# An mLSTM and HGRN2 decoder layer in one kernel: the mLSTM's fourfold key rows go through DRAM

## The chip, the cores and the metric

The kernel runs on one core of a Trainium2 chip. The metric is device time in microseconds (us), the median of several executions. Before the change it was 2313.5 us (three runs, 2311.78 to 2313.61).

## The reference

One inference step of one decoder layer, for a prompt of 256 new tokens and for 8 sequences of 8 new tokens each (the samples), 320 tokens in all, in float32. Two token mixers run on the same input: an mLSTM with 4 heads (keys of 256, values of 512) and an HGRN2 with 8 heads. Cut to the mLSTM:

```python
def step(carry, xs):
    C, n, m = carry
    ...
    s = jnp.einsum('bhtk,bhsk->bhts', qc, kc) * d
    num = jnp.einsum('bhts,bhsv->bhtv', s, vc) + w_inter[..., None] * jnp.einsum('bhtk,bhkv->bhtv', qc, C)
    den = jnp.sum(s, axis=-1) + w_inter * jnp.einsum('bhtk,bhk->bht', qc, n)
    h = num / jnp.maximum(jnp.abs(den), jnp.exp(-m_t))[..., None]
    ...
    C_new = decay[..., None, None] * C + jnp.einsum('bhs,bhsk,bhsv->bhkv', w_end, kc, vc)
    n_new = decay[..., None] * n + jnp.einsum('bhs,bhsk->bhk', w_end, kc)
    return (C_new, n_new, m_new), h
```

A large input projection stands before the mixers; branch projections, sigmoid gates, an output projection, LayerNorm, a feed-forward net (relu squared, 2048 to 8192 and back) and a second LayerNorm stand behind them. For the change only `C_new` of the samples matters: for each of 8 sequences and each head the sum over its 8 tokens of (weighted key) x (value), a 256x512 matrix.

## The kernel before

**Main stream.** All large products are written as 304 weight tiles of 128 output channels and 2048 input channels (`TILES`), each in two halves ("units", 128x1024 floats). float32 is got from float32r matmuls: a unit is loaded by DMA into `wr` (3 buffers, queue SP), ACT copies it to `wh` (the high part) and DVE subtracts to get `wl` (the low part, L478). Three matmuls (hi x hi, hi x lo, lo x hi) for each 128x128 block make 48 main matmuls a tile, 14592 in all, nearly all from L335 (`mm`). The activations stay in SBUF (`xh`, `xl`).

**Side work.** Everything else is written as Python generators (chains) that yield one instruction at a time with an estimated cost: ("pe", cost, fn), ("dve", ...), ("act", ...), ("sp", ...). A planner (`Sched`) runs while the program is built. It keeps an estimated clock for each engine; after every third main matmul `pump` lets the chains emit what would be ready by that clock. A PE instruction of a chain is emitted only when its inputs are estimated to be ready 450 ns before (`PE_LAT`). Chains wait on events (`Ev`, a planned time) and take buffers from pools (`acq`, `rel`). On the chip every engine, and every DMA queue, then runs its instructions in the order in which they were emitted, and waits on semaphores wherever the data are not there yet. So the plan sets the order; if the chip is later than the plan, an engine stands. All loads and stores but a few are issued by SP through one line (L338): weights (`wr<-wt`), the samples' states in and out (`C`, `Cs`), spills.

**The mLSTM heads.** The tiles of a head come as four value tiles, two key tiles, two query tiles and two gate tiles. They take the first 345 us or so for the four heads. For each head:

- `m_V` transposes the value tiles to token rows (L927). The samples' 64 token rows are split into a high part and a low part (`vs`). Then `copies_to` writes each of them into a DRAM tile `vsDm` twice, at row offset r of each sequence's 32 rows (four DMAs, one for each r), and `copies_from` reads the whole back as `vst`: "fourfold rows", 32 rows for each sequence. The planner books 5.0 us for the writes to land and 6.0 us for the read.
- `m_KW` multiplies the key tiles with the weights W (L979, L981) into `kw`, two tiles of 320 tokens, transposes the prompt's 256 tokens (four transposes, L986) and splits them into `khl` (ACT, then DVE at L991), which `m_CP` writes to DRAM (`kD`, beside `vD` for the values) for the end of the program. Then it sums the samples' keys (L1000 to L1002) and makes the keys' fourfold rows without DRAM: for each of the two key tiles `stack` (ACT and DVE, L950) writes the 64 sample tokens four times beside each other (high, low, high, low) into `st` (128x256), and two transposes (L1012) put them into a PSUM bank, 4 transposes a head. One ACT instruction (128x512) evicts the bank to `kst`, and the event KS is set.
- `m_sample` and `m_update` wait for KS and for `vst`, and make the state sums: `m_sums`, small matmuls (32 rows, 32x512) of `kst` with `vst`, whose 32 rows carry high x high, low x high, high x low and low x low. DVE adds them to the decayed state (L1238), and SP stores it.

`m_KW` of a head waits for KS of the head before; a buffer of `qk` becomes free at S, KS and QW.

Of the kernel before, what the change touches and what calls it, by code (L numbers as in the profile page):

```python
# [8 lines left out]
F32 = mybir.dt.float32  # L9
F32R = mybir.dt.float32r  # L10
# [3 lines left out]
ALU = mybir.AluOpType  # L14
# [8 lines left out]
MH, DK, DV = 4, 256, 512  # L23
# [207 lines left out]
def wait(*evs):  # L231
    return ("wait", evs)


def acq(pool, n=1):
    return ("acq", pool, n)


def rel(pool, item):
    return ("rel", pool, item)  # L240


def post(ev):
    return ("set", ev)


def act(n, psum=False, ptr=0):
    return ((61 if psum else 112) + n) / 1.2 + 93 * ptr


def dve(n, psum=False, mode=1, ptr=0):
    return ((62 if psum else 66) + n / mode) / 0.96 + 55 * ptr
# [10 lines left out]
PE_T = 112.0  # L263
# [28 lines left out]
class Program:  # L292
# [48 lines left out]
    def carve(self):  # L341
        class Part:
            def __init__(self, ap, lo=0):
                self.ap, self.o, self.end = ap, lo, ap.shape[1]

            def __call__(self, n, parts=128):
                self.o += n
                assert self.o <= self.end, (self.o, self.end)
                return self.ap[:parts, self.o - n:self.o]

            def three(self, a, b):
                return self(a * b).rearrange("p (a b) -> p a b", a=a)

        self.Part = Part
        A, B, C, R = Part(self.f1), Part(self.f2), Part(self.f3), Part(self.ra[:, 0:6400])

        self.hs = Pool([A(2048) for _ in range(3)])

        self.qk = Pool([A.three(4, 320) for _ in range(2)])
        self.vr = Pool([A.three(4, 320)])  # L360
        self.kw = Pool([B.three(2, 320)])
        self.bc = Pool([B(712) for _ in range(2)])
        self.eb0 = B(512)
        self.eb = Pool([self.eb0])
        self.stg = Pool([B(256) for _ in range(2)])
        self.qn0 = B(256)
        self.qn = Pool([self.qn0])
        X = Part(self.rx)
        self.cb = Pool([C(512) for _ in range(6)] + [X(512) for _ in range(8)])
        self.hb0 = C.three(3, 512)  # L370
        self.hb = Pool([self.hb0])
        self.qz0 = C(512)
        self.qz = Pool([self.qz0])
        self.tst = Pool([B(320) for _ in range(2)])
        self.tst2 = B(320)
        self.shl = Pool([(R(384), R(384), R(256))])
        self.vhl = Pool([R(2048).rearrange("p (x s v) -> p x s v", x=2, s=2)])
        self.vs = Pool([R(512)])
        self.khl = Pool([R(1024).rearrange("p (x s k) -> p x s k", x=2, s=2)])
        self.kst = Pool([R.three(2, 256)])  # L380
        self.vst = Pool([R.three(2, 512)])

        A, B, R = Part(self.f1, 6144), Part(self.f2), Part(self.rh)
        self.sb = Pool([A.three(4, 256) for _ in range(2)])
        self.at = Pool([A(512) for _ in range(2)])
        self.yb0 = A(1024)
        self.yb = Pool([self.yb0])
        self.it2 = [B.three(3, 256) for _ in range(2)]
        self.it = Pool(self.it2)
        self.hstg0 = [B(128) for _ in range(2)]  # L390
        self.hstg = Pool(self.hstg0)
        self.on0 = B.three(3, 256)
        self.on = Pool([self.on0])
        self.ho = Pool([B(320) for _ in range(2)])
        R2 = Part(self.ra, 5120)
        self.hkst = Pool([R2.three(2, 128)])
        self.phl = Pool([(R2(512), R2(512))])
        self.hvst = Pool([R.three(2, 256)])
        self.late = [B(320) for _ in range(4)]
        self.ats0 = B(128)  # L400
        self.ats = Pool([self.ats0])
        self.sg = Pool([Part(self.f2, 4960)(320), self.tst2])
        B = Part(self.f2, 4304)
        self.sr = Pool([B(320) for _ in range(2)])
        B = Part(self.f2, 3840)
        self.xr = Pool([B(320) for _ in range(4)])
        B = Part(self.f2)
        self.lnb = [B(320) for _ in range(7)]
        self.tmp = Pool([B(320) for _ in range(3)])
# [404 lines left out]
    def m_start(self, h):  # L814
        m = self.mh[h]
        self.qk.free.sort(key=lambda x: x[0])
        m["qk"] = self.qk.free.pop(0)[1]
        for n in ("q", "k"):
            m[n] = [Ev(), Ev()]
        m["v"] = [Ev() for _ in range(4)]  # L820
        for n in ("E", "S", "Vt", "Vs", "KW", "KH", "KS", "N", "CP", "QW", "bc_", "vst", "S0", "C", "ld"):
            m[n] = Ev()
        s = self.s
        s.spawn(self.m_E(h), 2)
        s.spawn(self.m_S(h), 2)
        s.spawn(self.m_KW(h), 3)
        s.spawn(self.m_V(h), 2)
        s.spawn(self.m_num(h), 2)
        s.spawn(self.m_CP(h), 4)
        m["parts"], m["inter"] = ([Ev() for _ in range(2 * NB)] for _ in range(2))  # L830
        m["cbs"] = []
        s.spawn(self.m_sample(h), 3)
        s.spawn(self.m_states(h), 3)
        for name, evs, pool in (("qk", ("S", "KS", "QW"), self.qk), ("eb", ("N", "S0"), self.eb), ("shl", ("N", "S0"), self.shl),
                                ("vhl", ("N", "CP"), self.vhl), ("vs", ("S0", "vst"), self.vs), ("kst_", ("QW", "KS"), self.kst), ("vst_", ("QW", "vst"), self.vst)):
            s.spawn(self.m_done(h, name, evs, pool), 3)

# [99 lines left out]
        m["vst_"] = vst  # L937
        yield from self.copies_from(self.vsDm[h], vst, m["vst"])

    def stack(self, st, src, his):  # L940

        v = self.nc.vector
        w = st.rearrange("p (b r t) -> p b r t", r=4, t=8)
        x = src.rearrange("p (b t) -> p b t", t=8).unsqueeze(2).to_broadcast([128, 8, 2, 8])
        step = his[1] - his[0]
        los = [r for r in range(4) if r not in his]
        pick = lambda rs: w[:, :, rs[0]:rs[0] + 2 * step - (step - 1):step, :]
        hi, lo = pick(his), pick(los)
        yield ("act", act(128), lambda: self.A(hi.bitcast(F32R), x))
        yield ("dve", dve(128), lambda: v.tensor_tensor(lo.bitcast(F32R), x, hi, ALU.subtract))  # L950

    def copies(self, hi, lo, to, his, st, ev):

# [15 lines left out]
    def m_KW(self, h):  # L969
        nc, v, m = self.nc, self.nc.vector, self.mh[h]  # L970
        if h:
            yield wait(self.mh[h - 1]["KS"])
        yield wait(*m["k"], self.rows_ev, m["bc_"])
        qk = m["qk"]
        W = m["bc"][:, 320:640]
        kw = yield acq(self.kw)
        for c in range(2):
            k = qk[:, 2 + c, :]
            yield ("dve", dve(256), lambda: v.tensor_tensor_reduce(  # L979
                kw[:, c, 0:256], k[:, 0:256], W[:, 0:256], 1.0, 0.0, ALU.mult, ALU.add, self.np_o[:, 2 * h + c:2 * h + c + 1]))  # L980
            yield ("dve", dve(64), lambda: v.tensor_tensor(kw[:, c, 256:320], k[:, 256:320], W[:, 256:320], ALU.mult))  # L981
        khl = yield acq(self.khl)
        b = yield acq(self.sbank)
        for i in range(2):
            for c in range(2):
                yield ("pe", PE_T, lambda: nc.tensor.transpose(b[:, 256 * i + 128 * c:256 * i + 128 * c + 128], kw[:, c, 128 * i:128 * i + 128], self.ident))  # L986
        m["khl"] = khl
        kh, kl = khl[:, 0], khl[:, 1]
        bv = b.rearrange("p (a k) -> p a k", a=2)
# [5 lines left out]
        n0, ns = self.n0[:, h], self.ns_o[:, h]  # L995
        sm = yield acq(self.sm)
        tm = sm[:, 0:16].rearrange("p (c b) -> p c b", c=2)
        kv = kw[:, :, 256:320].rearrange("p c (b t) -> p c b t", t=8)
        dc = m["bc"][:, 704:712]
        yield ("dve", dve(128), lambda: v.tensor_reduce(tm, kv, AX.X, ALU.add))  # L1000
        yield ("dve", 90, lambda: v.tensor_tensor(ns, n0, dc.unsqueeze(1).to_broadcast([128, 2, 8]), ALU.mult))
        yield ("dve", 90, lambda: v.tensor_tensor(ns, ns, tm, ALU.add))  # L1002
        yield rel(self.sm, sm)
        kst = yield acq(self.kst)
        m["kst_"] = kst
        b = yield acq(self.sbank)
        bv = b.rearrange("p (g k) -> p g k", g=2)
        for c in range(2):
            st = yield acq(self.stg)
            yield from self.stack(st, kw[:, c, 256:320], (0, 2))  # L1010
            for g in range(2):
                yield ("pe", PE_T, lambda: nc.tensor.transpose(bv[:, g, 128 * c:128 * c + 128], st[:, 128 * g:128 * g + 128], self.ident))  # L1012
            yield rel(self.stg, st)
        yield rel(self.kw, kw)
        yield ("act", act(512, True), lambda: self.A(kst, bv))
        yield rel(self.sbank, b)
        yield post(m["KS"])

    def ln_post(self, h, i, src, den, hb, parts, psum):

# [898 lines left out]
    def run(self, pool):  # L1919
# [10 lines left out]
        self.kD = [self.dr.tile([128, 2, 2, 256], F32, name=f"kD{j}") for j in range(MH)]  # L1930
        rows = lambda name, n, k: [self.dr.tile([32 * NB, k], F32, name=f"{name}{j}") for j in range(n)]
        self.ksD, self.vsD = rows("ksD", HH, HK), rows("vsD", HH, HV)
        self.vsDm = rows("vsDm", MH, DV)
        self.vD = [self.dr.tile([128, 2, 2, 512], F32, name=f"vD{j}") for j in range(MH)]
        self.ln = [dict(c=Ev(), x=Ev(), end=Ev(), pre=Ev(), m=Ev(), fin=Ev(), s=[Ev() for _ in range(KT)]) for _ in range(2)]
        self.xq, self.xq_ev = [None] * KT, [Ev() for _ in range(KT)]
# [83 lines left out]
```

## Time and profile before

| what | value |
|---|---|
| median of 3 runs | 2313.5 us |
| time of the profiled execution | 2313.08 us |
| its span, first to last instruction | 2311.3 us |
| mean granted clock of TensorE | 0.999 |
| DMA, mean rate over the span | 188 GB/s |
| L1012, transposes of the stacked keys | 16, 272 ns median, 75.2 to 331.9 us |
| L986, transposes of the prompt's keys | 16, 271 ns median, 64.0 to 317.9 us |
| DVE waiting for ACT's copies of weights (wl <- wh) | 443.0 us in 391 waits |
| SP waiting for L478 (weight buffers) | 817.8 us in 285 waits |

The page of a profile gives the busy time of each engine (PE is TensorE, PEld its weight loads, DVE VectorE, ACT ScalarE, POOL GpSimd), the chain of work that ended last, followed back from the last instruction, and the costliest groups of instructions by line of the kernel. Idle time of an engine that is off that chain costs nothing. A group's line has the operation, what it writes and reads (out<-in), the shape, how many there were, busy time and mean duration, and after the second bar the idle time ahead of it and what ended it. The views that answer a question add: waits (who waited for whom, how long in all, how often, the longest), stretches of time with each engine's busy time, instructions of one line or tile, and the timeline.

### The profile page before, as it was taken

The page shows a single profiled execution, that of the slowest core. Times are in us where ns is not written, and L with a number is a line of the kernel's source. Part 1 is how long each engine was busy: PE and PEld are TensorE (multiplying, and loading weights), DVE is VectorE, ACT ScalarE, POOL GpSimd, SP SyncE. Part 2 cuts the span into 40 slices and gives each one's busy share as a digit, 9 for nine tenths or more (in the row PEclk, how much of TensorE's full clock was granted, in tenths as well). Part 3 has the DMA queues.
Part 4 walks back from the last instruction along what each step waited for, and adds up shares of the span by engine and source line. Part 5 has one row for each costly group of instructions (what it writes and reads, how often), then busy time and mean ns, then how long its engine had stood idle before and what let it go on. Part 6 is the DMA issues. An engine that isn't in the chain of part 4 may idle for free.

```text
span 2311.3 us, 38984 instructions
## 1 busy us (share of the span) xinstructions
PE 2301.8 (100%) x15704; PEld 2259.0 (98%) x15704; DVE 1387.9 (60%) x2418; ACT 1040.0 (45%) x1649; POOL 12.2 (1%) x44
## 2 busy tenths in 40 slices
PE   9999999999999999999999999999999999999998
PEld 8999999999999999999999999999999999999998
DVE  6566567677777776555555767544554455445555
ACT  5444445454555555444433446533442344234434
POOL 0000000000000000000000000000000000000000
PEclk9999999999999999999999999999999999999999
DMA  6888686665666554555555644444444444444465
GB/s 214 286 303 267 232 302 219 201 216 194 197 201 226 190 193 166 180 172 173 174 170 183 217 158 146 148 153 146 147 153 148 148 151 149 147 149 151 146 228 182
DMA packets 155357, 434.96 MB, mean 188 GB/s; under 512 B 17436, under 2 KB 47268, under 8 KB 154152
## 3 DMA queue, kind: packets, MB, share of 16 engines
q1 hardware_dynamic: 154024, 426.18, 55.0%
q0 software_dynamic: 1152, 6.29, 0.8%
q8 instruction: 123, 2.02, 0.4%
q14 instruction: 58, 0.48, 0.1%
HBM read 376.25 MB, written 56.15 MB: 187 GB/s over the span
## 4 chain that ended last, share of the span: by engine, by line
PE 95%; DMA 2%; ACT 1%; DVE 1%; SPq 0%; issue 0%; ACTq 0%
PE bank L335 94%; DMA wr<-wt 2%; ACT f3m L329 0%; DMA Cs<-f 0%; DVE wl L478 0%; ACT wh L329 0%; PE bank L1602 0%; SPq L338 0%; DVE bb L478 0%; PE bank L1174 0%; ACT bb L329 0%; PE bank L927 0%; DMA f<-C 0%; PE bank L1438 0%; ACT oC L329 0%
## 5 line engine op out<-in xcount | busy, mean ns | idle before, releaser
L478 DVE TENSOR_TENSOR wl<-wr,wh 128x1024 fp32r<-128x1024 f32 x423 | 518.4, 1226 | 444.0 <-ACT wh L329 443.0
L335 PE MATMUL bank<-xh,wh 128*128 128x320 f32 (+1 forms) x2408 | 782.2, 325 | 0.4 <-ACT wh L329 0.4
L335 PE MATMUL bank<-xh,wl 128*128 128x320 f32 (+1 forms) x2408 | 746.1, 310 | 0.5 <-DVE wl L677 0.4
L335 PE MATMUL bank<-xl,wh 128*128 128x320 f32 (+1 forms) x2408 | 743.9, 309 | 0.0
L329 ACT ACTIVATE wh<-wr 128x1024 fp32r<-128x1024 f32 (+1 forms) x428 | 450.9, 1053 | 460.3 <-PE bank L335 432.4
L335 PEld LDWEIGHTS bank<-xh,wh 128*128 128x128 f32 x2408 | 453.8, 188 | 9.0 <-issue 3.4
L335 PEld LDWEIGHTS bank<-xl,wh 128*128 128x128 f32 x2408 | 454.3, 189 | 3.5
L335 PEld LDWEIGHTS bank<-xh,wl 128*128 128x128 f32 x2408 | 453.5, 188 | 1.0 <-DVE wl L677 1.0
L478 DVE TENSOR_TENSOR bb<-wr,bb 128x1024 fp32r<-128x1024 f32 x179 | 219.4, 1226 | 231.7 <-ACT bb L329 231.5
L335 PE MATMUL bank<-xh,bb 128*128 128x322 f32 x1280 | 287.2, 311 | 0.0
L335 PE MATMUL bank<-ra,bb 128*128 128x320 f32 x1264 | 283.6, 309 | 0.0
L329 ACT ACTIVATE bb<-wr 128x1024 fp32r<-128x1024 f32 x179 | 188.8, 1055 | 202.4 <-PE bank L335 191.6
L335 PE MATMUL bank<-rxb,bb 128*128 128x320 f32 x1112 | 255.0, 309 | 0.0
L335 PE MATMUL bank<-ra,wh 128*128 128x320 f32 x892 | 250.0, 309 | 0.0
L335 PEld LDWEIGHTS bank<-xh,bb 128*128 128x128 f32 x1280 | 215.9, 188 | 0.0
L335 PEld LDWEIGHTS bank<-ra,bb 128*128 128x128 f32 x1264 | 210.6, 188 | 0.2
L335 PE MATMUL bank<-xl,bb 128*128 128x322 f32 x640 | 198.7, 310 | 0.0
L335 PEld LDWEIGHTS bank<-rxb,bb 128*128 128x128 f32 x1112 | 188.4, 188 | 0.2
L335 PE MATMUL bank<-rxb,wh 128*128 128x320 f32 x596 | 184.3, 309 | 0.0
L335 PE MATMUL bank<-rxb,wl 128*128 128x320 f32 x596 | 183.9, 309 | 0.0
L329 ACT ACTIVATE f<-f,misc 128x320 f32<-128x320 f32 x210 | 118.0, 562 | 140.4 <-DVE f L1869 128.8
L335 PEld LDWEIGHTS bank<-ra,wh 128*128 128x128 f32 x892 | 161.5, 188 | 1.1 <-DVE ra L1632 0.9
(273 smaller groups left out, 2229.2 us busy)
## 6 DMA issues: line engine op xcount, KB each, us to landing
wr<-wt SPq DMA_DIRECT2D x602, 512.0 KB
rx<-C SPq DMA_DIRECT2D x36, 256.0 KB
Cs<-rx SPq DMA_DIRECT2D x36, 256.0 KB
f<-C SPq DMA_DIRECT2D x28, 256.0 KB
Cs<-f SPq DMA_DIRECT2D x28, 256.0 KB
vD<-ra SPq DMA_DIRECT2D x4, 1024.0 KB
f<-S SPq DMA_DIRECT2D x8, 512.0 KB
f3h<-S SPq DMA_DIRECT2D x8, 512.0 KB
```

The costliest lines, as they stand in the source:

```text
L329: return self.nc.scalar.activation(out, in_, func, **kw)
L335: self.nc.tensor.matmul(*a, **kw)
L478: self.V().tensor_tensor(lo, raw, hi.bitcast(F32), ALU.subtract)
```

## The change

The keys' fourfold rows are made as the values' are. `kw` becomes one tile of 640 columns: prompt tokens of key tile 0, the 64 sample tokens of tile 0, the 64 of tile 1, prompt tokens of tile 1. So the sample tokens of both key tiles are 128 adjacent columns, and one transpose turns them all. It is emitted ahead of the prompt's four. Two ACT copies and two DVE subtractions (each 64 rows of 128) put high and low parts into a new tile `ks` (in a part of `ra` that was not used), a new chain `m_KS` writes them with four DMAs to a DRAM tile `ksDm` and reads `kst` back. `stack`, its buffers `stg`, four transposes and an ACT eviction a head are gone. `m_KW` ends with a new event KW, for which the next head and the `qk` buffer wait in place of KS. Buffers in `f2` lie at other offsets.

```diff
-        self.kw = Pool([B.three(2, 320)])
+        self.kw = Pool([B(640)])
...
-        self.stg = Pool([B(256) for _ in range(2)])
...
+        self.ks = Pool([self.ra[:, 6400:6656]])
...
-    def stack(self, st, src, his):
...
-        yield ("act", act(128), lambda: self.A(hi.bitcast(F32R), x))
-        yield ("dve", dve(128), lambda: v.tensor_tensor(lo.bitcast(F32R), x, hi, ALU.subtract))
+    def pairs(self, src, b, to, n):
+        nc, v = self.nc, self.nc.vector
+        for p in range(n):
+            yield ("pe", PE_T, lambda: nc.tensor.transpose(b[:, 128 * p:128 * p + 128], src[:, 640 * p + 256:640 * p + 384], self.ident))
+        w = to.rearrange("q (p e k) -> q p e k", e=2, k=128)
+        up, dn = slice(0, 64), slice(64, 128)
+        for e, (h, l) in enumerate(((up, dn), (dn, up))):
+            x, hi, lo = b[h, 0:128 * n].rearrange("q (p k) -> q p k", k=128), w[h, :, e, :], w[l, :, e, :]
+            yield ("act", act(128 * n, True), lambda: self.A(hi, x))
+            yield ("dve", dve(128 * n, True), lambda: v.tensor_tensor(lo, x, hi.bitcast(F32), ALU.subtract))
...
     def m_KW(self, h):
         nc, v, m = self.nc, self.nc.vector, self.mh[h]
         if h:
-            yield wait(self.mh[h - 1]["KS"])
+            yield wait(self.mh[h - 1]["KW"])
...
+        ks = yield acq(self.ks)
+        b = yield acq(self.sbank)
+        yield from self.pairs(kw, b, ks, 1)
+        yield rel(self.sbank, b)
+        t = self.s.t["dve"]
+        self.s.spawn(self.m_KS(h, ks), 3, t)
         khl = yield acq(self.khl)
         b = yield acq(self.sbank)
...
-        kst = yield acq(self.kst)
-        m["kst_"] = kst
-        b = yield acq(self.sbank)
-        bv = b.rearrange("p (g k) -> p g k", g=2)
-        for c in range(2):
-            st = yield acq(self.stg)
-            yield from self.stack(st, kw[:, c, 256:320], (0, 2))
-            for g in range(2):
-                yield ("pe", PE_T, lambda: nc.tensor.transpose(bv[:, g, 128 * c:128 * c + 128], st[:, 128 * g:128 * g + 128], self.ident))
-            yield rel(self.stg, st)
-        yield rel(self.kw, kw)
-        yield ("act", act(512, True), lambda: self.A(kst, bv))
-        yield rel(self.sbank, b)
-        yield post(m["KS"])
+        yield rel(self.kw, kw)
+        yield post(m["KW"])
+
+    def m_KS(self, h, ks):
+        m = self.mh[h]
+        yield from self.copies_to(ks[64:128], ks[0:64], self.ksDm[h], (0, 2))
+        yield rel(self.ks, ks)
+        kst = yield acq(self.kst)
+        m["kst_"] = kst
+        yield from self.copies_from(self.ksDm[h], kst, m["KS"])
```

## The prediction

> **What bounds the kernel now.** I read the head of the page first: who is busy, and who is on the chain that ended last.
>
> ```profile
> span 2311.3 us, 38984 instructions
> PE 2301.8 (100%) x15704; PEld 2259.0 (98%) x15704; DVE 1387.9 (60%) x2418; ACT 1040.0 (45%) x1649; POOL 12.2 (1%) x44
> ...
> PE 95%; DMA 2%; ACT 1%; DVE 1%; SPq 0%; issue 0%; ACTq 0%
> ```
>
> TensorE is busy for all but 9.5 us of the span, most of that at the two ends. So time falls only if TensorE gets less to do, and rises only if it has to stand. Next, the waits of PE alone: after the first 26 us the longest is this one.
>
> ```profile
> PE bank L1012 <- DVE f L950: 0.4, 1, 0.4
> ```
>
> It belongs to the code that the change removes. Third, the groups by line, and the chain of waits between 324 and 333 us, for what a transpose really costs.
>
> ```profile
> L1012 PE MATMUL bank<-cst,f 128*128 128x128 f32 x16 | 4.4, 275 | 0.4 <-DVE f L950 0.4
> ```
>
> ```profile
> 327.11 0.11 PE bank L1012
> ...
> 330.40 0.11 PE bank L1174
> 330.51 0.11 PE bank L1012
> ```
>
> A transpose lasts 275 ns by itself, but transposes and matmuls overlap, and the chain charges each with 0.11 us. The timeline of PE shows the same:
>
> ```profile
> 326.65 0.31 PE L335 MATMUL bank<-xl,wh 128*128 128x320 f32 x1
> 326.80 0.31 PE L335 MATMUL bank<-xh,wl 128*128 128x320 f32 x1
> 326.94 0.27 PE L1012 MATMUL bank<-cst,f 128*128 128x128 f32 x1
> 326.97 0.39 PE L335 MATMUL bank<-xh,wh 128*128 128x320 f32 x1
> 327.20 0.31 PE L335 MATMUL bank<-xl,wh 128*128 128x320 f32 x1
> ```
>
> Two main matmuls without anything between them start 0.15 us apart (326.65, 326.80). From 326.80 to 327.20 there are two such steps and one transpose: 0.40 - 0.30 = 0.10 us. I take 0.11.
>
> Fourth, the four stretches in which the mLSTM heads make their keys, for the DMA engines that the change loads, and the DMAs of the value rows, which already go the way that the key rows are to go.
>
> ```profile
> core 0: us, PE busy (x) PEld busy (x) DVE busy (x) ACT busy (x) POOL busy (x), PEclk, DMA share, GB/s
> 58.00:85.00 27.00, 27.00 (x191) 24.95 (x191) 16.11 (x36) 12.18 (x20) 0.00 (x0) 1.00 0.98 363
> 142.00:168.00 26.00, 26.00 (x188) 23.91 (x186) 13.81 (x29) 13.10 (x24) 0.00 (x0) 1.00 0.89 324
> 230.00:256.00 26.00, 26.00 (x187) 23.83 (x186) 13.84 (x29) 12.69 (x24) 0.00 (x0) 1.00 0.76 254
> 312.00:345.00 33.00, 32.63 (x231) 29.84 (x229) 19.72 (x38) 15.26 (x28) 0.00 (x0) 1.00 0.90 319
> ```
>
> ```profile
> L338 SPq DMA_DIRECT2D vsDm<-ra x16: 575/586/1476, 59.6 to 322.8; - x16
> L338 SPq DMA_DIRECT2D ra<-vsDm x4: 371/709/1066, 71.1 to 328.7; - x4
> ```
>
> ```profile
> SPq L338 <- DMA vsDm<-ra: 4.8, 4, 3.9
> ```
>
> PE is full in all four (but for 0.4 us in the last), and the DMA engines nearly so in the first (0.98). The last fence: SP, the queue that issues every weight load, stood 4.8 us in four waits until value rows had landed in DRAM, once for 3.9 us.
>
> **The change part by part.** *Transposes.* Each head loses four at L1012 and gains one: 4 x 3 = 12 fewer, 12 x 0.11 = 1.3 us off TensorE. It is always full, so all of it lies on the path. Bounds: nearest rows of transposes that stand alone between main matmuls run from 0.11 to 0.20 us each, so 1.3 to 2.4. I take 1.3, since the chain charges that in three rows of three.
>
> The Trainium skill (TensorE: Matmul & The Clock Gate, Part 4: PE-mode transpose) gives about 275 ns for a 128x128 transpose inside a kernel. The group's mean here is just 275, but that is how long one lasts. Priced by it, the 12 would bring an estimated 3.3 us; the chain's 0.11 says they don't.
>
> *The stall.* The 0.4 us wait at 325.89 goes with L950: that DVE instruction stood behind a weight split (wl, 324.41 to 325.63) which a late weight load had delayed. In its place the single transpose waits for L981, an instruction after which L986 already transposes today at 314.8 without standing. I take -0.4; from 0 if a neighbour inherits it.
>
> *ACT and DVE.* Out per head: two ACT copies of 128x128 (0.30 us each), one ACT eviction of 128x512 (0.60), two DVE subtractions (0.29). In: two ACT copies and two subtractions of 64x128 from PSUM, 0.27 and 0.29 by the rows of L1491's kind. ACT saves 0.66 us a head, DVE nothing. Both are idle nearly half the time, so 0. The four copies now stand ahead of the prompt's transposes (L986), which move back by some 2 us; behind them are the DMAs to kD and vD, read only at the end of the program. 0. The next head's key work waits for KW, earlier than KS: heads lie over 80 us apart, 0.
>
> *DMAs.* Per head four writes of 64 KB and one read of 256 KB, 0.5 MB. At the 363 GB/s of the first stretch that is 1.4 us of all engines; in the other stretches there is room. They take SP 4 x 0.58 + 0.4 = 2.7 us. Behind them wait weight loads and state loads. What covers them: by the timeline, each weight half is split (end of wl) at least 4.0 us before its first matmul; in the four stretches 4.1 to 9.2. So 2.7 us are hidden, and even 2.7 + 1.4 very nearly. Were the cover gone, they would cost at most 4.1 - 4.0 in the worst place: 0 to 0.1 a head. I take 0.
>
> *The new wait.* The first of the small sums of a head (m_sums, 32x512 matmuls) needs kst, now from DRAM. Time for it, from the head's first key transpose to its first sums: 19.2, 22.5, 22.7 and 23.2 us (63.9 to 83.1, 144.3 to 166.9, 232.7 to 255.4, 314.9 to 338.1). What it needs, by the value rows: some 2.5 for the four copies (1.1 busy and the queueing behind a 1.23 us split), 3.0 to 6.9 from first to last write issue, 4.8 to 7.0 from there to the read, 0.4, and the planner's 6.0 + 0.6 until PE may use it: 17.3 to 23.4, some 20 likely. So in head 0 the key rows are about last, in the others there are some 3 us to spare. That the planner puts sums later costs nothing, as PE gets main matmuls instead. It costs only where the real read is later than planned, for then PE stands, and all main matmuls with it. Bounds: 0, and for a landing of 7.64 us (the longest in the chain here, "DMA Cs<-f" from 310.64) 7.64 - 6.6 = 1.0 a head, 4.2 in all. I take 0, since the value rows' reads (used 4.7 to 12 us after issue) made PE stand nowhere.
>
> Sum: -1.3 - 0.4 = -1.7 us against the profiled execution, whose own time is 2313.08 (span 2311.3 and 1.8 around it): 2311.4. The median of the runs, 2313.5, lies 0.4 above that execution, so 2311.8 is forecast: 0.07% less. No change that is measurable, as I count under 0.2% (4.6 us) as none: it is about what a measurement of this kernel can tell from no change.
>
> **The rivals.** *The gain is taken back.* One or two heads stand for kst by about 1 to 2 us, above all head 0, where the DMA engines are full and spare time is least; the net is -0.7 to +2.5: 2312.8 to 2316. For it: 0.98 share and 17.3 to 23.4 against 19.2. Against: the value rows in the same stretch.
>
> *The key rows come late, slower.* The place is SP's read of ksDm, which waits in the queue until four writes have landed. The planner books 5.0 us. Head 2's value rows took 3.9 more. A read that starts 3.9 us late makes PE stand 3.9 us at the first sums, once the spare time there is used up. Two such heads cost 7.8 - 1.7 = +6.1: 2319.6; all four 15.6 - 1.7 = +13.9: 2327. It decides from 3.2 us of late landing per head in two heads (4.6 + 1.7 = 6.3 us in all). For it: key and value writes now queue together in full DMA stretches, and SP's two waits add up ahead of weight loads with 4.1 us of cover. Against: three of the four waits of today were together 0.9 us, and heads 1 to 3 have some 3 us to spare.
>
> The Trainium skill (DMA: Bandwidth & Descriptors, Anatomy of one DMA) speaks for this rival: completion "can cause a surprisingly long delay especially when the write target is HBM"; its constant is some 2 us. The trace has 4.8 to 7.0 us from last write to read, part of which is the planner's. By that constant alone no head would be late, and 2311.8 would stand.
>
> *More than the count says.* Twice the stall and transposes at 0.2 give 2.4 + 0.8 = 3.2 us, still within 0.2%. Faster by 4.6 us has no place in the trace; what remains is a new order of work that happens to suit.
>
> **How the numbers follow.** Forecast 2311.8: 0.55. Taken back: 0.22. Late key rows: 0.18. More than the count, past 0.2%: 0.05. So faster 0.05, same 0.55 + 0.22 = 0.77, slower 0.18. Range: below, 2.4 + 0.4 off the profiled time gives 2310.3 and I let it reach 2309.8; above, up to the two-headed case, 2319. What is left out is the 0.05 below and about half of the late case.
>
> **What would show it.** Right: one key-row transpose a head in place of four, PE's idle time after 26 us near zero, no row "PE bank <- DMA ra<-ksDm". Taken back: that row with 1 to 2 us at the first sums of head 0 (about 83 us). Late: that row with 3 us or more, and SP waiting for "DMA ksDm<-ra" over 3 us a time. I am wrong if the clock row moves from 1.00, if main matmuls wait for wl, or if the new order of work leaves PE standing far behind the mLSTM heads, which no row here lets me see.

## The result and the profile after

The changed kernel is slower: 2318.85 us, the median of 17 runs (2315.43 to 2323.56), against 2312.58 us for the kernel before in 17 runs beside it (2311.33 to 2313.91). The ratio is 1.0027 with a 95% interval of 1.002 to 1.0033: 4.6 to 7.6 us. Its spread is also three times that of before, 8.1 us against 2.6.

The head of the page after:

```profile
span 2318.0 us, 38988 instructions
PE 2303.0 (99%) x15692; PEld 2260.4 (98%) x15692; DVE 1388.2 (60%) x2418; ACT 1038.3 (45%) x1645; POOL 12.2 (1%) x44
...
PE 97%; DMA 1%; ACT 1%; DVE 0%; issue 0%; SPq 0%; ACTq 0%; DVEq 0%
```

PE has the 12 instructions fewer that the change promised (15704 to 15692), and yet 1.2 us more busy time, and the span is 6.7 us longer. The busy time that is not work but a slower clock is explained below; the rest is standing. The waits of PE (who waited for whom: us in all, times, the longest):

```profile
PE bank L335 <- DMA ra<-ksDm: 3.7, 1, 3.7
PE bank L335 <- ACT wh L329: 2.0, 1, 2.0
PE bank L335 <- DVE f L1733: 1.2, 1, 1.2
```

The first row is new: once, the small sums of a head waited 3.7 us for the key rows from DRAM. The second is at 10 us, the start of the program (0.4 before); it is 1.8 in an experiment below that is not slower, so it belongs to the execution and not to the change. The third is the sum for LayerNorm at 1300 us (L1727 before, 0.3 there). The wait for L950 is gone. The one transpose a head has the length that was expected; instructions of its line:

```profile
L947 PE MATMUL bank<-cst,f x4: 270/272/329, 65.3 to 323.9; 128*128 128x128 f32 x4
```

Where the 3.7 us lie, and what follows them, shows in the timeline of PE in head 1:

```profile
169.14 1.46 PE L335 MATMUL bank<-rx,f 128*32 128x512 f32 x10
174.28 0.80 PE L335 MATMUL bank<-ra 32*128 32x512 f32 x4 [3.69 <-DMA ra<-ksDm]
175.01 0.64 PE L335 MATMUL bank<-xh,wh 128*128 128x320 f32 x1
175.45 0.47 PE L335 MATMUL bank<-xl,wh 128*128 128x320 f32 x1
175.72 0.47 PE L335 MATMUL bank<-xh,wl 128*128 128x320 f32 x1
```

Behind the wait the same main matmuls last 0.47 us where they lasted 0.31, and start 0.27 us apart where they started 0.15 apart. The stretches around it say why (PEclk is the granted clock):

```profile
165.00:170.00 5.00, 5.00 (x41) 3.90 (x40) 3.75 (x7) 3.90 (x9) 0.00 (x0) 1.00 1.03 356
170.00:175.00 5.00, 1.31 (x12) 0.29 (x4) 0.00 (x0) 0.00 (x0) 0.00 (x0) 0.84 1.01 407
175.00:180.00 5.00, 5.00 (x23) 4.86 (x20) 3.29 (x4) 1.06 (x1) 0.00 (x0) 0.50 0.46 169
180.00:185.00 5.00, 5.00 (x35) 4.57 (x34) 3.00 (x5) 3.23 (x6) 0.00 (x0) 0.97 0.82 279
```

Still during the wait TensorE's granted clock falls to a half; by the trace's clock record it stays there from 173.4 to 180.3 us, 6.8 us. Six of them fall on work, which costs some 3.0 us. So the wait costs twice: 3.7 + 3.0 = 6.7 us. The Trainium skill (TensorE: Matmul & The Clock Gate, Why this matters for your kernels) warns of just this: no gaps over some 3 us between matmuls. The trace agrees at 3.69 us; the limit itself is tried below.

The chain of waits names what led up to it (start, us, what), and SP's timeline the order of the DMAs:

```profile
160.77 4.71 DMA ksDm<-ra
...
165.86 8.38 DMA ra<-ksDm
```

```profile
163.24 0.42 SPq L338 DMA_DIRECT2D wr<-wt  x1
163.77 0.40 SPq L338 DMA_DIRECT2D kD<-ra  x1
164.22 0.52 SPq L338 DMA_DIRECT2D vD<-ra  x1
165.86 0.37 SPq L338 DMA_DIRECT2D ra<-ksDm  x1
```

The last key write took 4.7 us to land, within the 5.0 booked. The read took 8.38 us from issue to landing, where the planner books 6.0 and PE's 0.6 on top. Right ahead of it SP had issued kD and vD, 1.5 MB, which at the 400 GB/s of this stretch are 3.8 us of all DMA engines.

The slow landing alone would not have made PE stand. In the same planned piece of PE's work (`m_sample`, booked as `PE_C`, 2.0 us) other products stand ahead of the sums; in the trace they take from 168.67 to 170.60. So the plan left the read at least 0.62 for its issue, 6.0, 0.6 and 1.9, some 9.1 us, between its issue and the sums. PE was there 4.74 us after the issue (170.60 less 165.86). By these bookings SP issued the read at least 4.4 us late against PE, and it is both together that make 3.7: 4.4 + 8.4 - 9.1. With a landing of 5.0 the same sum leaves 0.3. Where SP lost its time is not settled: between 138 and 170 us it stood 6.0 us for stores of states to land (`Cs<-rx`; 2.5 in the kernel before), but 6.6 in experiment 8, where PE does not stand.

Laying the n-th main matmul of one trace beside the n-th of the other gives the balance: the changed kernel is 1.0 us behind at 34 us (the start), 0.9 at 155, 6.2 at 676, 5.7 at 1290 and 6.5 at 1308 us. Head 1's wait and the clock make up the step in the middle (+6.7, less some 1.4 saved on transposes and the old stall), and 0.8 is lost at LayerNorm (0.2 in the second profile, experiment 11).

### The profile page after: what moved, and what is told of

Read it like the earlier page. It is cut to its first block, busy times and chain, and to the rows that moved or that the text cites. A ratio compares the mean times of both kernels' runs of the same rounds, so it can differ in the third digit from the quotient of the medians.

```text
span 2318.0 us, 38988 instructions
## 1 busy us (share of the span) xinstructions
PE 2303.0 (99%) x15692; PEld 2260.4 (98%) x15692; DVE 1388.2 (60%) x2418; ACT 1038.3 (45%) x1645; POOL 12.2 (1%) x44
## 4 chain that ended last, share of the span: by engine, by line
PE 97%; DMA 1%; ACT 1%; DVE 0%; issue 0%; SPq 0%; ACTq 0%; DVEq 0%
PE bank L335 96%; DMA wr<-wt 0%; ACT f3m L329 0%; DMA ra<-ksDm 0%; PE bank L1608 0%; PE bank L927 0%; PE bank L1180 0%; DMA ksDm<-ra 0%; PE bank L1444 0%; ACT oC L329 0%; SPq L338 0%; DVE bb L478 0%; ACT wh L329 0%; PE bank L996 0%; PE bank L1557 0%
```

## The experiments

The theory: the key rows' read lands later than it is booked, PE stands in the order of the plan, and the clock falls. The rivals: the added DMA traffic costs time by itself; or the new order of work does.

**1. The booking alone.** One number of the planner:

```diff
-        yield from self.copies_from(self.ksDm[h], kst, m["KS"])
+        yield from self.copies_from(self.ksDm[h], kst, m["KS"], 11000.0)
```

(`copies_from` books that in place of 6000.)

> The changed kernel, with one number of the planner different: it books 11 us instead of 6 for the read of the key rows. Theory (PE stands in head 1 because the read lands 8.4 us after its issue where 6.0 are booked, and TensorE's clock then falls to a half for 6.8 us): no wait of PE for ksDm, granted clock 1.00 throughout, and about 2311 to 2312.5 us, 0 to 2 below the kernel before. Rival (the added DMA traffic or the new order costs time whatever PE waits for): still some 4 us or more above the kernel before.

Measured: 2314.21 us against 2313.23 for the kernel before (ratio 1.0002, interval 0.9993 to 1.0011). No wait for ksDm is left, and the clock stays at 1.00. The loss is gone, within that interval, with no DMA and no instruction taken away: what cost time was the wait, with the clock's fall behind it. The median lies 1.7 us above the upper end of what I expected, so the gain isn't there either.

**2. kD and vD behind the read.**

```diff
-        yield wait(m["KH"], m["Vt"])
+        yield wait(m["KH"], m["Vt"], m["KS"], m["vst"])
```

> The changed kernel, with the writes of kD and vD (1.5 MB a head) planned after the fourfold rows have come back. Theory (in head 1 the read stands behind these 1.5 MB on the DMA engines, 3.8 us at the 400 GB/s moved there): the read lands within the 6 us booked, PE does not wait for ksDm, 2311 to 2312.5 us. Rival (the read is late because of the weight and state loads around it, or because SP issues it late): PE still waits 2 us or more for ksDm in some head, and the time stays at 2315 or more.

Measured: 2312.45 us (ratio 1.0, interval 0.9991 to 1.0009). No wait for ksDm in the profile, at the old booking of 6 us. Two of 11 runs were at 2317, though. A read that is late now and then would explain them, but no trace of such a run was kept; experiment 3, whose sums need no key rows from DRAM, has one at 2317.75 too, and the kernel before reaches 2315.9 in the runs beside it. Its waits of PE begin with

```profile
PE bank L335 <- DVE f L1733: 1.0, 1, 1.0
```

which is the LayerNorm sum again, taken up in experiment 8.

**3. The traffic alone.** In the kernel before, a chain beside `m_KW` writes 64 rows of `khl` four times and reads 256 KB back into a tile that nothing uses:

```diff
+    def m_X(self, h):
+        x = self.mh[h]["khl"][:, 0, 0, :]
+        yield from self.copies_to(x[64:128], x[0:64], self.ksDm[h], (0, 2))
+        yield from self.copies_from(self.ksDm[h], self.spare, Ev())
...
+        self.s.spawn(self.m_X(h), 3, self.s.t["dve"])
```

> The kernel before, its key rows still made by four transposes a head, with DMAs of the changed kernel's shapes added (four writes of 64 rows of 1 KB to DRAM, one read of 256 KB back into a tile that nothing reads). Theory (the traffic itself is covered; only the wait costs): 2312.5 to 2314, within 1 us of the kernel before, no new wait of PE over 0.5 us. Rival (traffic in full DMA stretches delays weights and states): 4 us or more slower, with PE or the weight splits waiting for loads.

Measured: 2312.66 us (ratio 0.9999, interval 0.999 to 1.0008). SP even waited 15.8 us for these writes to land (us in all, times, the longest), and no wait of PE names a load:

```profile
SPq L338 <- DMA ksDm<-ra: 15.8, 5, 5.9
```

The first rival falls: the 0.5 MB a head and SP's 2.7 us are covered, as the prediction had it.

**4. The price of a transpose.** In the kernel before, each transpose of L1012 is issued four times (`for _ in range(4)`).

> The kernel before, each of its 16 transposes of stacked keys issued four times in place of once: 48 more transposes, nothing else. Theory (a transpose takes 0.11 us of the stream on PE): 5.3 us slower, 2317.9. Rival (it takes the 0.27 us that it lasts): 13 us slower, 2325.6.

Measured: 2318.27 us, 5.04 above the kernel before (ratio 1.0023, interval 1.0014 to 1.0032). That is 0.105 us for each of the 48 (0.07 to 0.15 by the interval), not 0.27. By this, 12 fewer are worth 1.3 us.

**5. A booking in between.** As 1, with 8000.0.

> The changed kernel with 8 us booked for the read of the key rows, between the 6 of the change and the 11 of e1_book11. Theory (PE stands for what the read takes beyond the booking, and the clock falls only after a long stand): a wait of PE for ksDm of 1 to 2.5 us in head 1 or none, granted clock 1.00 throughout, and 0 to 2 us over e1_book11. Rival (any stand costs a fixed price, or the wait does not follow the booking): a wait of 3.5 us or more, the clock at a half for some 6 us, 2317 or more.

Measured: 2314.87 us (ratio 1.001, interval 1.0 to 1.0019), with seven runs from 2314.3 to 2315.3 and three from 2318.8 to 2319.2. The profile is of one of the three, and shows two waits, 0.53 us in head 1 and one in head 3:

```profile
348.37 0.80 PE L335 MATMUL bank<-ra 32*128 32x512 f32 x4 [3.08 <-DMA ra<-ksDm]
```

With it the clock went to a half from 348.1 for 6.8 us. I had expected no wait over 2.5 us and no fall of the clock, and missed: in head 3, where the read stood behind kD and vD as well, it took 9.0 us from issue to the sums. The two groups of runs, 4 us apart, fit a wait that comes in some executions; only the one profile shows it.

**6. Standing on purpose.** In the kernel before, in the feed-forward part: a matmul, n fills by GpSimd, a matmul that needs them, for n from 1 to 12.

```diff
+            self.mm(b[:, 0:1], x[:, 0:128], one, start=True, stop=True)
+            for _ in range(n + 1):
+                pool.memset(x[:, 0:640], 1.0)
+            self.mm(b[:, 1:2], x[:, 0:128], one, start=True, stop=True)
```

(The code counts its n from 0.)

> The kernel before, with twelve stands of TensorE made on purpose in the feed-forward part, where weights lie ready 20 us ahead: a small matmul, then n fills of a tile by GpSimd (128x640, some 0.6 us each), then a small matmul that needs them, with n from 1 to 12, some 56 us apart. Theory (TensorE's clock falls to a half only after a stand of between 0.5 us, which the kernel before has without a fall, and 3.7 us, and stays low for some 6 us once it works again): short stands show a clock of 1.00 and cost their own length, long ones a stretch at 0.5 and some 3 us more. Rival (the halved clock of the changed kernel had another cause): clock 1.00 throughout and about 55 us longer, the sum of the stands.

Measured: 2396.19 us, 82.8 above the kernel before, where PE stood for 55.2 us in all. The timeline for n of 1, 2, 3, 5 and 12 (PE's idle time in brackets):

```profile
1513.77 0.38 PE L335 MATMUL bank<-misc,f 128*128 128x1 f32 x2 [0.80 <-POOL f L613]
...
1572.20 0.38 PE L335 MATMUL bank<-misc,f 128*128 128x1 f32 x2 [1.50 <-POOL f L613]
...
1633.11 0.38 PE L335 MATMUL bank<-misc,f 128*128 128x1 f32 x2 [2.19 <-POOL f L613]
...
1757.68 0.59 PE L335 MATMUL bank<-misc,f 128*128 128x1 f32 x2 [3.56 <-POOL f L613]
...
2217.08 0.59 PE L335 MATMUL bank<-misc,f 128*128 128x1 f32 x2 [8.39 <-POOL f L613]
```

and the 10 us behind each of these:

```profile
1515.00:1525.00 10.00, 10.00 (x71) 10.00 (x70) 3.01 (x4) 3.19 (x3) 0.00 (x0) 1.00 0.45 145
1572.00:1582.00 10.00, 9.80 (x57) 9.80 (x58) 2.34 (x3) 2.12 (x2) 0.15 (x1) 0.83 0.32 106
1633.00:1643.00 10.00, 9.89 (x57) 9.90 (x58) 2.39 (x4) 3.58 (x6) 0.05 (x1) 0.83 0.29 105
1757.00:1767.00 10.00, 9.32 (x44) 9.32 (x45) 1.22 (x1) 1.06 (x1) 0.63 (x1) 0.66 0.14 49
2217.00:2227.00 10.00, 9.92 (x54) 9.92 (x55) 1.72 (x3) 2.54 (x4) 0.03 (x1) 0.78 0.15 52
```

0.80 us leave the clock at 1.00; every stand from 1.50 us on brings it to a half, for 3.4, 6.8 or 10.2 us by the clock record. By the main matmuls of the two traces, laid side by side, such a stand costs 2.1 to 3.4 us beyond its own length; 0.6 of that the stand of 0.80 costs too, without a fall. (In all 82.8 less 55.2 is 27.6 us.) The stands of 3.56 and 4.25 us cost 7.0 and 6.4 in all, so 6.7 for a wait of 3.7 us is what such a wait costs here whatever causes it. In this run the limit lies between 0.80 and 1.50 us, inside the 0.5 to 3.7 that I had named; the low clock lasted 3.4 to 10.2 us, not some 6 each time.

**7. The prompt first.** In the changed kernel, the call of `pairs` and the start of `m_KS` are moved behind `post(m["KH"])`.

> The changed kernel with the single transpose and its copies put behind the prompt's transposes and their split, where the stacked keys stood before. Theory (which DMAs stand between SP and the read decides): the key rows start some 3 to 6 us later and kD and vD earlier; the planner puts the first sums later in step, so the stand of PE depends on whether kD and vD still come just ahead of the read: if they are issued 4 us or more before it, no wait over 1 us and 2311.5 to 2313.5; if just ahead, a wait like the change's. Rival (the early place of the transpose is what avoids worse): slower than the changed kernel, over 2319.

Measured: 2318.22 us (ratio 1.0019, interval 1.001 to 1.0028), like the changed kernel. kD and vD are issued at 158.1 and 159.8 in head 1, long before the key read at 171.62, which lands in 5.87 us; and still PE stands 2.97 us there (and 1.31 in head 3, without a fall of the clock). My condition (kD and vD 4 us ahead, so no wait) was wrong. SP's timeline has the reason:

```profile
159.81 1.08 SPq L338 DMA_DIRECT2D vD<-ra  x1
160.99 0.90 SPq L338 DMA_DIRECT2D wr<-wt  x1
161.93 1.41 SPq L338 DMA_DIRECT2D vsDm<-ra  x1
163.44 4.08 SPq L338 DMA_DIRECT2D ksDm<-ra  x3
```

Behind kD these issues take SP 0.9 to 1.4 us each in place of some 0.6, and what follows is issued later. The planner books 0.62 for each. This read landed within its booking, so the stand is SP's lateness alone. That kD and vD cause the slow issues is a reading and not shown: of the 24 issues over 0.85 us between 30 and 350 us of the kernel before, 14 lie within 8 us behind kD or vD, and 10 elsewhere. The early place of the transpose shows neither help nor harm.

**8. LayerNorm's sum later.** Experiment 2, and

```diff
- ... (self.s.t["dve"] + 600.0,))
+ ... (self.s.t["dve"] + 2200.0,))
```

> e2_kd_after with one more number of the planner changed: the sum over channels of LayerNorm (a matmul with ones) is planned 2.2 us after DVE's estimate in place of 0.6, so that main matmuls fill the time. Theory (what the saved transposes bring is given back at 1292 us, where PE stands 1.0 to 1.3 us for DVE's sum, 0.3 in the kernel before): that wait is gone and the time is 0.7 to 1.0 us under e2_kd_after, some 1.5 to 2 under the kernel before. Rival (the sum then comes late for the tiles behind it, or another wait takes its place): no gain over e2_kd_after.

Measured: 2312.64 us (ratio 0.9998, interval 0.9989 to 1.0006). In the trace the wait for L1733 is down to 0.2 us, and between 1290 and 1308 us nothing is lost, where experiment 2 loses 0.7. The medians show none of it (0.77 under the kernel before here, 0.78 in experiment 2). By the trace the wait is gone, as the theory says; in the runs I can't tell it from nothing. It also repeats experiment 2's finding: here the read lands in

```profile
164.74 5.00 DMA ra<-ksDm
```

5.00 us, against 8.38 with kD and vD right ahead. The packet records have every read (256 rows of 1 KB): in the four heads of the changed kernel the last row comes 6.7 to 7.9 us after the issue, in experiments 2 and 8 2.7 to 6.1. But there is no spare time even so: here the read lands at 169.73, and PE had ended its other products just then.

**9. All three remedies.** Experiment 8, with 8 us booked for the read.

> The changed kernel with the three remedies together: kD and vD planned after the fourfold rows, 8 us booked for the key read, LayerNorm's sum planned 2.2 us after DVE. Theory: no wait of PE for ksDm in any execution, so no execution near 2316 to 2319, and 2311.3 to 2312.3, 1 to 2 us under the kernel before. Rival (the saved transposes bring nothing): within 0.5 us of the kernel before.

Measured: 2312.21 us against 2313.17 (ratio 0.9995, interval 0.9986 to 1.0004), and no run of 11 over 2312.94, while every other variant of the change has some at 2315 to 2320. The kernel before has some at 2315.5 beside it, so a high run is not always a late key read. In the profile PE waits for ksDm no more. It is the best version of all, 0.96 us under the kernel before in the median, but the interval includes no change. In the profiled execution the clock fell at the program's start as well, after a stand of 1.27 us, and main matmuls were 1.7 us behind those of the kernel before at 34 us; from there to 1308 us they gain 2.8.

**10. The read on another queue.**

```diff
+        eng = self.nc.sync if q == "sp" else self.nc.gpsimd
+        t = yield (q, 620, lambda: eng.dma_start(st.bitcast(F32), to.rearrange("(g p) k -> p g k", g=2)))
...
+        yield from self.copies_from(self.ksDm[h], kst, m["KS"], "pool")
```

(The value rows keep "sp".)

> The changed kernel with the read of the key rows issued on GpSimd's queue in place of SP's, the writes still on SP's. Theory A (the read is late because it stands in SP's queue, behind kD, vD and weights, and behind SP's slow issues): it lands within 6 us of its issue, PE does not wait for ksDm, 2311.5 to 2313.5. Theory B (the DMA engines are full in that stretch, whatever the queue): PE waits 1 us or more for ksDm in head 1 or 3, 2315 or more.

Measured: 2312.79 us (ratio 0.9998, interval 0.9989 to 1.0008). Neither theory is quite right. The read lands no sooner, as its row of DMA issues says (KB each, median us to landing):

```profile
ra<-ksDm POOLq DMA_DIRECT2D x4, 256.0 KB, 8.0
```

So the queue is not what makes it slow to land, and A fails there; that fits full engines (share 0.97 from 165 to 172 us), as B has it. In head 1 PE stands only 0.8 us, without a fall of the clock, since the read is issued at 161.74, not 165.86. But that is not the other queue's doing: the last key write, still SP's, was issued at 156.46 in place of 160.77, and in both runs the read follows it by 5.1 to 5.3 us. Why SP was earlier there is not shown.

**11. The change again**, for a second profile.

> The changed kernel once more, unchanged, for a second profile: the first had one wait of 3.7 us, in head 1, while its executions spread over 8 us. Theory (the landing of the read varies from one execution to the next): PE waits for ksDm again in head 1, 1 to 6 us, perhaps in head 0 or 3 too, with the clock at a half behind each wait over some 1.5 us. Rival (the loss sits elsewhere and the wait was an accident of one profile): no wait for ksDm, and still 2316 or more.

Measured: 2319.59 us, one execution. The wait is in head 1 again:

```profile
174.53 0.80 PE L335 MATMUL bank<-ra 32*128 32x512 f32 x4 [4.81 <-DMA ra<-ksDm]
```

The read from 166.64 takes 7.85 us behind kD and vD, and the clock is at a half for 6.8 us from 174.0. The rival falls.

## Why the prediction was wrong, point by point

- *Transposes, -1.3 us.* Right: 12 fewer, at 0.105 us by experiment 4.
- *The stall, -0.4 us.* Right as far as it goes: L950's wait is gone, L947 waits at most 0.2 us in its place.
- *The traffic, 0.* Right as far as it costs time by itself: experiment 3. *ACT and DVE, 0:* no run tests them alone; ACT's busy time fell from 1040.0 to 1038.3 us, DVE's stayed (1387.9 and 1388.2).
- *The moved kD and vD, 0.* Wrong. "Behind them are the DMAs to kD and vD, read only at the end of the program. 0." I asked who waits for these DMAs, not whom they make wait. Moved back with the prompt's transposes, they came to lie right ahead of the key read, in a stretch where the DMA engines were then full (1.03); experiments 2 and 8 take them away from there, and in 8 the read lands in 5.0 us in place of 8.4.
- *The new wait, 0.* Here the prediction failed: "I take 0, since the value rows' reads (used 4.7 to 12 us after issue) made PE stand nowhere." The wait came, 3.7 us once. The value rows were no measure, for none had both a large write ahead and a short time: in head 1 their read came 4.0 us behind vD, but was used 10 us after its issue; in head 2 it was used after 5.0, but came 11.5 us behind vD. The upper bound failed too: 1.0 us a head from a landing of 7.64 asks only how long the read takes, and left out that SP may issue it late against PE, by at least 4.4 us here. (On the other side it left out the 1.9 us of other products ahead of the sums, so that a landing of 8.38 alone would still have cost nothing.) I had set the least spare time in head 0; the wait came in head 1.
- *What a wait costs.* Every price was of the wait alone. The clock's fall adds 3.0 us to one wait of 3.7, so a single late head is enough: 6.7 - 1.7 is +5.0, with 0.8 at LayerNorm +5.8, and with the 1.0 that this execution lost at its start +6.8, where the spans differ by 6.7.
- *The rival "the key rows come late, slower".* Its outcome came: a read issued late, and PE standing at the first sums. Its path did not: it had the read wait until the writes have landed, over 3 us a time, but SP stood for them 2.1 us in all, 1.3 at the longest, and was late before it issued them. It also asked for two late heads, as it had no price for the clock.
- *Within 0.2%, with 0.77.* Wrong. Slower, with 0.18, came. That 2318.85 still lies inside the range, just under its upper end of 2319, is luck: the end was set by two late heads at 3.9 us each, and what came was one at 3.7 and a slower clock.
- *Slow completion of writes.* I had cited the Trainium skill (DMA: Bandwidth & Descriptors, Anatomy of one DMA) for this rival: a write to HBM can be slow to complete. It was not the cause in head 1: the last key write landed 4.7 us after its issue, within the 5.0 booked. The section describes GpSimd's path, moreover, and these writes went through SP's queue.

With the wait removed, the medians of experiments 2, 8 and 9 lie 0.8 to 1.0 us under the kernel before, that of experiment 1 lies 1.0 above it, and all their intervals include no change. Experiment 3, which saves no transpose, lies 0.6 under it. So the runs do not show the 1.7 us. In the traces of experiments 1 and 2 main matmuls run 2.0 and 2.3 us ahead of before at 1290 us, and 1.0 and 1.6 ahead at 1308: a part is given back where PE, now early, waits for DVE's sum behind a chain of weight loads.

## What to carry to other kernels

Where the order of work is fixed ahead, a data path whose latency is booked needs slack on the engine that is full: ask of every DMA that an edit moves not only who reads it, but what stands behind it in the queue, and how late the queue that issues it can run. Price a stand of TensorE at its length plus the clock's fall. And when an off-path chain has latency to spare, book it generously: 11 us in place of 6 cost nothing here that the runs can tell.

## What the runs showed of the hardware that was not expected

- TensorE's clock went to a half with idle times of 1.50 us and more in experiment 6, and of 2.97 us and more in the mLSTM heads; not with 0.80 and 1.31 us. At the start of the program, where PE also stands, it fell with 1.27 us (experiment 9) and 1.72 (experiment 7), but not with 1.82 (experiment 3) and 1.99 (the changed kernel). It stayed low for 3.4, 6.8 or 10.2 us, and stands of 3.56 and 4.25 us cost 3.4 and 2.1 us extra. So the length of a stand alone doesn't set it. The Trainium skill (TensorE: Matmul & The Clock Gate, Part 1: The HAM clock gate) has a window of some 3.4 us that runs free of the kernel. The steps agree: in experiment 6 the clock stays high for 58.03 us between stands, 17 times 3.41. Its limit of some 3 us of idle time does not: half of that was enough.
- Behind 1.5 MB of writes several DMA issues in a row took SP 0.9 to 1.4 us in place of 0.6 (experiment 7); that the writes are the cause is not shown.
- A read of 256 KB took 5.0 us from issue to landing in experiment 8, and 8.4 with 1.5 MB issued 2 us earlier; on another queue, with the same 1.5 MB ahead, it took 8.0.
